# Nearest-neighbour upsampling: one run of 512 rows per partition, two loads and ten stores, and no hold between them

## Chip, cores and metric

One core of one Trainium2 chip. The metric is the time of one execution in microseconds (us); the kernel before takes 199.01 us (median of 3 runs, 198.98 to 199.02). "Span" is the time from the first to the last instruction in a profiled execution, 1.6 to 1.8 us less than the time. Transfer sizes follow the profile: 4096 KB there is 4.194 MB.

## The reference

```python
# x: (16, 64, 64, 64) float32, scale_factor = 2
result = np.zeros((batch, channels, 2 * h, 2 * w), dtype=np.float32)
for i in range(new_h):
    for j in range(new_w):
        result[:, :, i, j] = x[:, :, i // 2, j // 2]
```

Each element is written four times: 16.78 MB are read and 67.11 MB written. As rows, x has 65,536 rows of 64 elements (256 B), and each becomes 256 elements (1 KB) of output.

## The kernel before

The input goes in quarters, 128 rows per partition in each. The last quarter's load is cut, so that 24 rows per partition come as a small piece of their own. VectorE expands 9/16 of a store's rows, ScalarE the rest, and SyncE issues every transfer. Eight stores have 32 rows and four have 64. The **hold**: the first store waits for the last load but one. Its data has been there for some 24 us by then, so this is a wait on purpose.

```python
    M4 = R // (4 * P)                      # 128 rows per partition in a quarter
    slots = [0, 2, 3, 1]
    TAIL = 24
    ...
    for n, slot in enumerate(slots):
        first = n * P * M4
        xt = mem[:, slot * WB : (slot + 1) * WB].rearrange("p (m w) -> p m w", m=M4)
        src = xf[first : first + P * M4, :].rearrange("(p m) w -> p m w", p=P)
        cuts = (0, M4 - TAIL, M4) if n == len(slots) - 1 else (0, M4)
        for lo, hi in zip(cuts, cuts[1:]):
            loads.append(nc.sync.dma_start(out=xt[:, lo:hi], in_=src[:, lo:hi]))
    ...
    def store(part, r0, k, at):
        kv = k * 9 // 16
        ...
        nc.vector.tensor_copy(out=u[:, :kv], in_=expanded(xp[:, r0 : r0 + kv, :]))
        nc.scalar.copy(out=u[:, kv:], in_=expanded(xp[:, r0 + kv : r0 + k, :]))
        dst = of[first : first + P * m, :].rearrange("(p m) w -> p m w", p=P)
        return nc.sync.dma_start(out=dst[:, r0 : r0 + k, :], in_=u)
    ...
    for n, (q, r0) in enumerate(small):
        st = store(q, r0, 32, WX + n % 2 * (WU // 2))
        if n == 0:
            tc.add_manual_dep(st.ins, loads[-2].ins.name, ...,
                reason="stores begin as the loads end")
```

## Time and profile before

| | before |
|---|---|
| time, median of 3 | 199.01 us |
| span | 197.4 us |
| busy: transfers / ScalarE / VectorE | 98.9% / 26% / 20% |
| transfers | 5 loads, 12 stores |

Read the transfers' share first: with 98.9% neither VectorE nor ScalarE can be the bound. Then the landings: how long after its issue each group of transfers has landed. This is the part of the page on issues, with size of one and median time to landing in us:

```profile
out_dram<-mem SPq DMA_DIRECT2D x8, 4096.0 KB, 16.2
mem<-in_x_dram SPq DMA_DIRECT2D x3, 4096.0 KB, 21.4
mem<-in_x_dram SPq DMA_DIRECT2D x1, 3328.0 KB, 38.1
mem<-in_x_dram SPq DMA_DIRECT2D x1, 768.0 KB, 39.4
```

The small last load lands 1.3 us further from its issue than the one before it.

### The profile page before, as it was taken

To read this page: it belongs to the slowest core of one execution; us is meant where nothing else is said; L and a number is where in the kernel's file an instruction comes from. 1 tells how busy PE (TensorE), PEld (TensorE's weight loads), DVE (VectorE), ACT (ScalarE), POOL (GpSimd) and SP (SyncE) were. 2 spreads that over 40 slices of the span, in tenths; PEclk is the share of its full clock that TensorE was granted. 3 is DMA by queue.
4 is the path that set the end of the run, shared out by engine and by line. 5 is a ranking of instruction groups with operands and counts; after the bars stand their busy time and mean duration, and the time that the engine had idled before them with its cause. 6 is when DMAs were issued, how large, how long until landed. Compare 5 with 4: busy or idle time off the path is not lost.

```text
span 197.4 us, 117 instructions
## 1 busy us (share of the span) xinstructions
DVE 40.2 (20%) x12; ACT 51.3 (26%) x13; POOL 0.2 (0%) x4
## 2 busy tenths in 40 slices
DVE  0045000000505059505050007200810091000000
ACT  2047000000505060606079107400840093000000
POOL 0000000000000000000000000000000000000000
DMA  8999999999999999999999999999999999999994
GB/s 319 425 425 425 438 445 418 411 452 451 432 425 438 425 432 432 425 432 425 425 425 425 425 425 425 478 505 438 438 438 438 438 438 425 425 425 425 425 425 212
DMA packets 2448, 83.89 MB, mean 425 GB/s; under 512 B 272, under 2 KB 272, under 8 KB 400
## 3 DMA queue, kind: packets, MB, share of 16 engines
q1 hardware_dynamic: 2448, 83.89, 98.9%
HBM read 16.78 MB, written 67.11 MB: 425 GB/s over the span
## 4 chain that ended last, share of the span: by engine, by line
DMA 71%; ACT 11%; SPq 1%; issue 0%; ACTq 0%
DMA out_dram<-mem 52%; DMA mem<-in_x_dram 19%; ACT mem L140 11%; SPq L124 0%; SPq L142 0%; ACTq L140 0%
## 5 line engine op out<-in xcount | busy, mean ns | idle before, releaser
L140 ACT COPY mem<-mem 128x3584 f32<-128x3584 f32 (+1 forms) x12 | 50.0, 4174 | 112.5 <-DMA out_dram<-mem 102.1
L139 DVE COPY mem<-mem 128x4608 f32<-128x4608 f32 (+1 forms) x12 | 40.2, 3360 | 123.1 <-DMA out_dram<-mem 110.6
L140 ACT ACT_TABLE_LOAD x1 | 1.3, 1283 | 0.8 <-PEq L178 0.8
L178 POOL MEMSET const-bfloat16-1.0<- 128x1 bf16 x1 | 0.1, 102 | 0.0
L178 POOL MEMSET const-uint8-127<- 128x1 uint8 x1 | 0.1, 101 | 0.0
L178 POOL MEMSET const-float32-0.0<- 128x1 f32 x1 | 0.1, 99 | 0.2 <-issue 0.2
L178 POOL MEMSET const-float32-1.0<- 128x1 f32 x1 | 0.1, 98 | 0.0
## 6 DMA issues: line engine op xcount, KB each, us to landing
out_dram<-mem SPq DMA_DIRECT2D x8, 4096.0 KB, 16.2
mem<-in_x_dram SPq DMA_DIRECT2D x3, 4096.0 KB, 21.4
mem<-in_x_dram SPq DMA_DIRECT2D x1, 3328.0 KB, 38.1
mem<-in_x_dram SPq DMA_DIRECT2D x1, 768.0 KB, 39.4
out_dram<-mem SPq DMA_DIRECT2D x4, 32.4
```

Source lines behind the costliest of these rows:

```text
L139: nc.vector.tensor_copy(out=u[:, :kv], in_=expanded(xp[:, r0 : r0 + kv, :]))
L140: nc.scalar.copy(out=u[:, kv:], in_=expanded(xp[:, r0 + kv : r0 + k, :]))
L178: nc = _bacc.Bacc("TRN2", target_bir_lowering=False, num_devices=1)
```

## The change

Its intent: fewer and longer transfers. Each partition owns 512 rows that follow one another, so any cut of its rows is a single run in memory. Two loads of 256 rows (64 KB per partition) replace five, and ten stores of 40 to 56 rows replace twelve. The stores are issued as soon as they are ready and stand in the queue behind the second load; the hold and the small last load go.

```diff
... (views of x and of the output added)
-    M4 = R // (4 * P)
-    slots = [0, 2, 3, 1]
-    TAIL = 24
+    rows = [40, 44, 44, 54, 54, 56, 56, 56, 56, 52]
+    FREE = 79
+    mem = mem_pool.tile([P, WF + R * W], fdt, name="mem")      # R = 512 here
+    xt = mem[:, WF:].rearrange("p (r w) -> p r w", r=R)
... (quarters, cuts and list of loads removed)
+    for lo in range(0, R, R // 2):
+        nc.sync.dma_start(out=xt[:, lo : lo + R // 2], in_=xp[:, lo : lo + R // 2])
... 
+    for n, k in enumerate(rows):
+        size = k * GROW * W
+        at = 0 if n % 2 == 0 else WF + r0 * W - size
...
+        kv = k * 9 // 16
+        nc.vector.tensor_copy(out=u[:, :kv], in_=expanded(r0, r0 + kv))
+        nc.scalar.copy(out=u[:, kv:], in_=expanded(r0 + kv, r0 + k))
+        nc.sync.dma_start(out=op[:, r0 : r0 + k, :], in_=u)
... (store() and its two loops removed)
-        if n == 0:
-            tc.add_manual_dep(st.ins, loads[-2].ins.name, ...)
```

The odd stores are built on top of input rows that are already expanded.

More of the change, by code (lines that the diff above doesn't have):

```diff
@@ L93 @@
     B, C, H, W = x.shape
-    R = B * C * H
+    R = B * C * H // P
     fdt = x.dtype
-    WX = R // P * W
-    WU = 16384
-    mem_pool = ctx.enter_context(tc.tile_pool(name="mem", bufs=1))
-    mem = mem_pool.tile([P, WX + WU], fdt, name="mem")
-    M4 = R // (4 * P)
-    slots = [0, 2, 3, 1]
-    TAIL = 24
-    WB = M4 * W
-    assert M4 * P * 4 == R and 2 * WB == WU
-    xf = x.rearrange("b c h w -> (b c h) w")
-    of = out.rearrange("b c (h hd) w -> (b c h) (hd w)", hd=s)
-    parts = []
@@ L117 @@
-    loads = []
-    for n, slot in enumerate(slots):
-        first = n * P * M4
-        xt = mem[:, slot * WB : (slot + 1) * WB].rearrange("p (m w) -> p m w", m=M4)
-        src = xf[first : first + P * M4, :].rearrange("(p m) w -> p m w", p=P)
-        cuts = (0, M4 - TAIL, M4) if n == len(slots) - 1 else (0, M4)
-        for lo, hi in zip(cuts, cuts[1:]):
-            loads.append(nc.sync.dma_start(out=xt[:, lo:hi], in_=src[:, lo:hi]))
-        parts.append([(xt, first, M4)])
-    def expanded(rows):
-        return rows.unsqueeze(2).unsqueeze(4).to_broadcast(
-            [P, rows.shape[1], s, W, s]
-        )
@@ L132, in store @@
-    def store(part, r0, k, at):
-        xp, first, m = part
-        kv = k * 9 // 16
-        u = mem[:, at : at + k * s * W * s].rearrange(
+    xp = x.rearrange("b c h w -> (b c h) w").rearrange("(p r) w -> p r w", p=P)
+    op = out.rearrange("b c (h hd) w -> (b c h) (hd w)", hd=s).rearrange(
+        "(p r) w -> p r w", p=P
+    )
+    rows = [40, 44, 44, 54, 54, 56, 56, 56, 56, 52]
+    GROW = s * s
+    FREE = 79
+    WF = FREE * GROW * W
+    assert sum(rows) == R
+    mem_pool = ctx.enter_context(tc.tile_pool(name="mem", bufs=1))
@@ new lines, with expanded @@
+    mem = mem_pool.tile([P, WF + R * W], fdt, name="mem")
+    xt = mem[:, WF:].rearrange("p (r w) -> p r w", r=R)
+    for lo in range(0, R, R // 2):
+        nc.sync.dma_start(
+            out=xt[:, lo : lo + R // 2], in_=xp[:, lo : lo + R // 2]
+        )
+    def expanded(r0, r1):
+        return (
+            xt[:, r0:r1].unsqueeze(2).unsqueeze(4).to_broadcast([P, r1 - r0, s, W, s])
+        )
+    r0 = 0
+    before = (0, 0)
+    for n, k in enumerate(rows):
+        size = k * GROW * W
+        at = 0 if n % 2 == 0 else WF + r0 * W - size
+        assert at >= before[1] or at + size <= before[0]
+        before = (at, at + size)
+        u = mem[:, at : at + size].rearrange(
@@ L137, in store @@
             "p (k a w b) -> p k a w b", k=k, a=s, w=W
         )
-        nc.vector.tensor_copy(out=u[:, :kv], in_=expanded(xp[:, r0 : r0 + kv, :]))
-        nc.scalar.copy(out=u[:, kv:], in_=expanded(xp[:, r0 + kv : r0 + k, :]))
-        dst = of[first : first + P * m, :].rearrange("(p m) w -> p m w", p=P)
-        return nc.sync.dma_start(out=dst[:, r0 : r0 + k, :], in_=u)
-    small = [(q, r0) for n in (0, 3) for q in parts[n] for r0 in range(0, q[2], 32)]
-    large = [(q, r0) for n in (1, 2) for q in parts[n] for r0 in range(0, q[2], 64)]
@@ L148 @@
-    for n, (q, r0) in enumerate(small):
-        st = store(q, r0, 32, WX + n % 2 * (WU // 2))
-        if n == 0:
-            tc.add_manual_dep(
-                st.ins,
-                loads[-2].ins.name,
-                mybir.DependencyInfo(
-                    mybir.DependencyClass.Sync, mybir.DependencyReason.DATA
-                ),
-                reason="stores begin as the loads end",
-            )
-    for n, (q, r0) in enumerate(large):
-        store(q, r0, 64, (0, WX)[n % 2])
+        kv = k * 9 // 16
@@ L165 @@
+        nc.vector.tensor_copy(out=u[:, :kv], in_=expanded(r0, r0 + kv))
+        nc.scalar.copy(out=u[:, kv:], in_=expanded(r0 + kv, r0 + k))
+        nc.sync.dma_start(out=op[:, r0 : r0 + k, :], in_=u)
+        r0 += k
 _INS = ['x', 'scale_factor']
```

## The prediction

> **What bounds the kernel now.** I read the page first: the busy shares, the row of DMA in the slices, and the part on DMA queues.
>
> ```profile
> span 197.4 us, 117 instructions
> DVE 40.2 (20%) x12; ACT 51.3 (26%) x13; POOL 0.2 (0%) x4
> ...
> DMA  8999999999999999999999999999999999999994
> GB/s 319 425 425 425 438 445 418 411 452 451 432 425 438 425 432 432 425 432 425 425 425 425 425 425 425 478 505 438 438 438 438 438 438 425 425 425 425 425 425 212
> DMA packets 2448, 83.89 MB, mean 425 GB/s; under 512 B 272, under 2 KB 272, under 8 KB 400
> ...
> q1 hardware_dynamic: 2448, 83.89, 98.9%
> ```
>
> The two engines that compute are busy for a fifth and a quarter of the span. The transfers are busy for 98.9% of it, and in all but the first and the last slice. So the kernel is a queue of transfers. Three things could make it shorter: a hole in the queue, a cost per transfer, or a higher rate. I looked for each.
>
> For that I need a clock of when transfers land. The timeline gives it: a copy that waited for a buffer starts when the store that held the buffer has landed.
>
> ```profile
> 12.49 5.03 DVE L139 COPY mem<-mem 128x4608 f32<-128x4608 f32 x2 [12.49 <-DMA mem<-in_x_dram]
> 39.86 125.06 SPq L142 DMA_DIRECT2D out_dram<-mem  x12
> 51.48 3.18 ACT L140 COPY mem<-mem 128x3584 f32<-128x3584 f32 x1 [32.73 <-DMA out_dram<-mem]
> ...
> 119.60 6.17 ACT L140 COPY mem<-mem 128x7168 f32<-128x7168 f32 x1 [10.09 <-DMA out_dram<-mem]
> ...
> 158.42 4.96 DVE L139 COPY mem<-mem 128x9216 f32<-128x9216 f32 x1 [14.47 <-DMA out_dram<-mem]
> ```
>
> Columns: start, busy time, engine, line, operation, shape, and in brackets the idle time before it with what ended it. The first load (4096 KB, which is 4.194 MB) lands at 12.49. The first store lands at 51.48 and the eighth at 119.60, since the second large expansion waits for that one. The last store is issued at 164.60 (timeline) and takes 32.53 us to land (last transfer piece of the chain in order of time), so it lands at 197.13.
>
> From this I work out three numbers:
> - A 4.194 MB store every (119.60 - 51.48) / 7 = 9.731 us.
> - An 8.389 MB store every (197.13 - 119.60) / 4 = 19.383 us.
> - Two small ones take 2 x 9.731 = 19.462, so a transfer has a fixed part of about 0.08 us; the rest is (19.383 - 0.08) / 8.389 = 2.301 us per MB, or 434.6 GB/s.
>
> The queue's start follows from the first load: 12.49 - 9.73 = 2.76 us. Now the check. If there were no hole anywhere, the end would be 2.76 + 83.886 x 2.301 + 17 x 0.08 = 2.76 + 193.02 + 1.36 = 197.14. The trace has 197.13. At the hold itself: five loads and one store are 20.97 MB, so the first store should land at 2.76 + 48.25 + 0.48 = 51.49; the trace has 51.48. **There is no hole at the hold**, nor elsewhere that I can see. The chain of waits does show 38.12 us of loads and then a store issued at 39.86, but the last load piece (768 KB, issued at 2.2, 39.4 us to landing) lands only at 41.6, so the store was in the queue before the queue ran dry.
>
> **What the Trainium skill says.**
> - "DMA: Bandwidth & Descriptors", section "Where 436 GB/s comes from": the ports of the 16 engines into the core's memory allow 435.2 GB/s. My 434.6 between landings agrees, so there is no rate left to gain.
> - The same page, "Queues, rings and completion order": on each engine descriptors are consumed in ring order. So a store issued while loads are still queued stands behind them and does not take their place. The trace of before agrees in order at least: the small last load landed at 41.6 and the store behind it at 51.48, one store's time later.
> - The same page, "Latency and other measured facts", on row pitch in HBM: with a pitch of 512 KiB from partition to partition copies ran at 207 GB/s, with 2 MiB at 164, where 214 was full. This bears on the change, as below; the trace of before, whose output pitch is 128 KB, can't show it.
> - "SBUF — State Buffer", "Who interferes with whom": DMA doesn't contend with the compute engines. Before agrees: the cadence of 9.73 us is the same for stores that have copies beside them all along.
>
> **The change part by part.**
>
> *Fewer transfers.* 5 loads become 2, 12 stores become 10: 17 transfers become 12. The bytes stay. 5 x 0.08 = 0.4 us less, all on the path, since the queue is the path. That is the whole certain gain.
>
> *No hold.* It takes away a wait that cost nothing (the check above). What happens instead: the first load is now 8.389 MB and lands at 2.76 + 19.30 + 0.08 = 22.1. Copy costs come from the groups by shape:
>
> ```profile
> L140 ACT COPY mem<-mem 128x3584 f32<-128x3584 f32 x8 | 25.3, 3178 | 75.9 <-DMA out_dram<-mem 65.5 <-DMA mem<-in_x_dram 10.4
> L140 ACT COPY mem<-mem 128x7168 f32<-128x7168 f32 x4 | 24.7, 6166 | 36.6 <-DMA out_dram<-mem 36.6
> L139 DVE COPY mem<-mem 128x4608 f32<-128x4608 f32 x8 | 20.4, 2559 | 77.3 <-DMA out_dram<-mem 64.8 <-DMA mem<-in_x_dram 12.5
> L139 DVE COPY mem<-mem 128x9216 f32<-128x9216 f32 x4 | 19.8, 4960 | 45.9 <-DMA out_dram<-mem 45.8
> ```
>
> The number after the bar is the group's busy time, then the mean of one in ns. ScalarE: (6166 - 3178) / 3584 = 0.834 ns per element plus 0.19 us. VectorE: (4960 - 2559) / 4608 = 0.521 ns plus 0.16 us. The first expansion has 40 rows, of which 18 for ScalarE, 18 x 256 = 4608 elements, 4.0 us. The first store is issued at about 26.3, the second (20 rows on ScalarE, 5120 elements, 4.5 us) at 30.8. Both wait in the queue for the second load, which lands at 2.76 + 38.61 + 0.16 = 41.5. So the queue holds 11 to 15 us of work ahead of them.
>
> *Does the queue stay full after that?* An expansion n needs the space of store n - 2, and runs while store n - 1 drains. The tightest case is a 44-row store (5.767 MB, 13.35 us) over the expansion of 54 rows (24 on ScalarE, 6144 elements, 5.3 us): 8 us to spare. The longest expansion (56 rows: 25 on ScalarE, 6400 elements, 5.5 us; 31 on VectorE, 7936 elements, 4.3 us) runs under a store of at least 54 rows, 16.4 us. The new buffers overlap rows of the input that are already expanded; those are waits between the two engines of at most a copy's length, hidden as well. Busy time of the engines hardly moves: 10 instructions each in place of 12, the same elements, so about 50 and 39 us.
>
> *Longer rows, other pitch.* Loads go from 32 KB rows that follow one another without a gap to 64 KB rows with a pitch of 128 KB. Stores go from 32 and 64 KB rows with a pitch of 128 KB to rows of 40 to 56 KB with a pitch of 512 KB. A longer row gains no more than is in the 0.08 above. The pitch is the one thing that could cost.
>
> *Ends.* The first load is still moved ahead of the barrier, and the closing is the same, so the 2.76 at the start and the time outside the span (199.01 - 197.4 = 1.6) stay.
>
> Sum: the queue ends at 2.76 + 193.02 + 12 x 0.08 = 196.7, and the time is 199.01 - 0.4 = 198.6.
>
> **The rivals.**
> 1. *The pitch slows the stores.* If the figure of the skill's page holds for the stores alone, they run at 207 / 214 of their rate: the 67.11 MB take 154.4 us now and would take 5.2 us more, so 203.8, just over 2% slower. For it: the slices show the packets of the engines bunched in time in the large-store stage (one microsecond 1049 GB/s, the next 0, around 128 us), so the engines do walk in step, which is what aliasing needs. Against it: that figure is for loads and stores at the same pitch and with short tiles, and here only the stores have it, a single direction at a time. I give a full cost of 2% or more 0.12, and a part of it 0.15.
> 2. *The hold paid for something*, as its author must have thought: stores in the queue early mix with loads and slow them, or delay the second load. For: it was put in on purpose. Against: ring order, and no copy needs the second load before the sixth expansion (rows 236 to 292), which waits for the fourth store, near 41.5 + 182 x 0.131 MB x 2.301 = 96 us. At most a microsecond.
> 3. *An engine becomes the bound at the start or a copy runs late.* The first expansion starts 10 us later than now. It has 15 us to spare, so it costs nothing; it would have to take four times as long to show.
> 4. *Faster by more than 2%* would need 4 us. The queue has 197.13 - 192.8 (83.886 MB at 435.2 GB/s) = 4.3 us above the port's limit, of which 2.76 is the start. I see no way to it.
>
> **Range and chances.** With 0.73 the time is 198.6 within half a microsecond; the pitch gives a tail upward to 204. I set the prediction a little above the sum, at 198.8, the range from 198.2 to 201.5. Faster 0.01, within 2% 0.87, slower 0.12.
>
> **What would show it right or wrong.** Right: 12 transfers, a DMA share of 98% or more, the first store issued near 26 us and landing near 53.6, landings of 56-row stores every 7.340 x 2.301 + 0.08 = 17.0 us, no slice in the middle below 420 GB/s. The pitch is at work if the 56-row stores land every 17.4 us or more, while the loads still land near 22.1 and 41.5. The hold's rival is at work if the second load lands well after 41.5. A copy is late if SyncE's queue issues a store after the one before it has landed.

## The result and the profile after

The changed kernel takes 199.12 us (median of 6 runs, 199.04 to 199.25), the kernel before 198.96 us in the same rounds. The ratio is 1.0009, with a 95% interval of 0.9996 to 1.0022: the same. A ratio here is the mean time of one kernel's fast runs over that of the other's of the same rounds, so not quite the ratio of the medians. Runs e1 to e4 were made on one chip and e5 to e11 on another, each with the kernel before beside them.

The page of the changed kernel, its lines on the span, busy shares, slices and queue:

```profile
span 197.3 us, 103 instructions
DVE 59.6 (30%) x10; ACT 52.1 (26%) x11; POOL 0.2 (0%) x4
...
GB/s 425 425 425 425 425 425 425 425 282 490 437 439 439 439 439 429 368 538 359 437 460 370 534 372 407 523 372 407 523 372 407 523 372 407 523 372 413 464 432 259
...
q1 hardware_dynamic: 1728, 83.89, 99.1%
```

Its timeline (columns as before):

```profile
25.88 146.81 SPq L139 DMA_DIRECT2D out_dram<-mem  x10
54.38 4.46 ACT L138 COPY mem<-mem 128x5120 f32<-128x5120 f32 x1 [24.04 <-DMA out_dram<-mem]
...
122.19 5.52 ACT L138 COPY mem<-mem 128x6400 f32<-128x6400 f32 x1 [3.08 <-DVE mem L137]
130.61 8.42 DVE L137 COPY mem<-mem 128x7936 f32<-128x7936 f32 x1 [8.51 <-DMA out_dram<-mem]
147.41 5.53 ACT L138 COPY mem<-mem 128x6400 f32<-128x6400 f32 x1 [19.70 <-DMA out_dram<-mem]
147.48 8.42 DVE L137 COPY mem<-mem 128x7936 f32<-128x7936 f32 x1 [8.45 <-DMA out_dram<-mem]
...
164.41 7.88 DVE L137 COPY mem<-mem 128x7424 f32<-128x7424 f32 x1 [8.51 <-DMA out_dram<-mem]
```

Three things are to be seen. The stores run at the predicted pace: 56-row stores land at 130.61, 147.48 and 164.41, 16.9 us apart. But the first store lands at 54.38 and not at the predicted 53.6, so something before it cost 0.7 to 0.8 us. And VectorE takes 8.42 us for 7936 elements, twice what I worked out. ScalarE waits for it twice, some 3.1 us each time (the line at 122.19 is one), but the stores are still in time: the copy that starts at 130.61 is done at 139.03, and the queue has work until the store ahead lands, at 147.4.

Where the 0.8 us went can be read from the windows, here of 1.5 us. A packet is a piece of a transfer; here it is the 64 KB of one partition. It is counted where it starts, so each window below holds the sixteen packets of one round, one per transfer engine. The last two columns are the transfers' share of engine time and GB/s:

```profile
35.00:36.50 1.50, 0.00 (x0) 0.00 (x0) 0.00 (x0) 1.00 1.61 699
37.50:39.00 1.50, 0.00 (x0) 0.00 (x0) 0.00 (x0) 1.00 2.34 699
```

Both windows start the same bytes. The first is a round in the middle of the second load: 1.61 x 1.50 = 2.42 us per packet. The second is that load's last round: 2.34 x 1.50 = 3.51 us. So **the last packets of the loads were stretched by 1.1 us** on average, just before the stores that were waiting behind them. The second load lands late too. The view of the loads' line gives the times from issue to landing of the two loads as least and greatest:

```profile
DMA to landing us min/median/max: 21.8/31.6/41.4
```

The second was issued at 0.8, so it landed at 42.2 where 41.5 was predicted.

### The profile page after: what moved, and what is told of

Read it like the earlier page. It is cut to its first block, busy times and chain, and to the rows that moved or that the text cites. A ratio compares the mean times of both kernels' runs of the same rounds, so it can differ in the third digit from the quotient of the medians.

```text
span 197.3 us, 103 instructions
## 1 busy us (share of the span) xinstructions
DVE 59.6 (30%) x10; ACT 52.1 (26%) x11; POOL 0.2 (0%) x4
## 4 chain that ended last, share of the span: by engine, by line
DMA 67%; DVE 13%; ACT 7%; issue 0%; DVEq 0%; SPq 0%; ACTq 0%
DMA out_dram<-mem 56%; DVE mem L137 13%; DMA mem<-in_x_dram 11%; ACT mem L138 7%; DVEq L137 0%; SPq L139 0%; ACTq L138 0%
## 5 line engine op out<-in xcount | busy, mean ns | idle before, releaser
L137 DVE COPY mem<-mem 128x7936 f32<-128x7936 f32 (+4 forms) x10 | 59.6, 5969 | 112.7 <-DMA out_dram<-mem 90.9
L138 ACT COPY mem<-mem 128x6400 f32<-128x6400 f32 (+4 forms) x10 | 50.8, 5077 | 108.3 <-DMA out_dram<-mem 82.3
```

Of the source, the lines that this page charges most:

```text
L137: nc.vector.tensor_copy(out=u[:, :kv], in_=expanded(r0, r0 + kv))
L138: nc.scalar.copy(out=u[:, kv:], in_=expanded(r0 + kv, r0 + k))
```

## The experiments

**My theory, called Q:** a store that stands in the queue while the last loads still run stretches those loads; the hold avoids this by putting the first store into the queue just as the loads end. **Rivals:** the small last piece is what makes the switch cheap, hold or no hold (C); the hold was idle, as I had predicted (H); the 512 KB pitch of the stores costs time (P).

| run | transfers | time us | kernel before us (same runs) | ratio (95% interval) |
|---|---|---|---|---|
| changed kernel | 12 | 199.12 | 198.96 | 1.0009 (0.9996 to 1.0022) |
| e1, before without hold | 17 | 199.40 | 198.94 | 1.0019 (1.0007 to 1.0032) |
| e2, changed + cut + hold | 13 | 198.75 | 198.94 | 0.9989 (0.9977 to 1.0002) |
| e3, changed + cut | 13 | 199.15 | 198.94 | 1.0009 (0.9997 to 1.0022) |
| e4, changed, even rows | 12 | 199.19 | 198.94 | 1.0012 (0.9998 to 1.0026) |
| e5, changed, unbroken stores | 12 | 199.24 | 198.97 | 1.0016 (1.0002 to 1.0030) |
| e6, changed, stores in four | 42 | 200.58 | 198.97 | 1.0081 (1.0068 to 1.0094) |
| e7, changed + hold of one, no cut | 12 | 205.57 | 198.97 | 1.0334 (1.0318 to 1.0350) |
| e8, changed + hold, cut of 64 rows | 13 | 199.18 | 198.97 | 1.0008 (0.9995 to 1.0021) |
| e9, changed + hold of two, no cut | 12 | 200.01 | 198.98 | 1.0051 (1.0037 to 1.0066) |
| e10, e2 + even rows | 13 | 198.81 | 198.98 | 0.9990 (0.9977 to 1.0003) |
| e11, changed + hold, cut of 12 rows | 13 | 205.45 | 198.98 | 1.0329 (1.0316 to 1.0342) |

### e1: the kernel before without its hold

```diff
-        if n == 0:
-            tc.add_manual_dep(st.ins, loads[-2].ins.name, ...)
```

> The kernel before without the wait of the first store; loads as before, the last piece of 24 rows too. Theory Q (stores that are queued while loads still run stretch the last load packets): the switch from loads to stores loses about 1 us, as in the changed kernel, so the first store lands near 52.5 instead of 51.5 and the time is 199.9 to 200.0. Rival C (the small last piece of the loads is what makes the switch cheap): first store lands at 51.5, time 199.0 within 0.15. Rival H (the hold was simply idle, as I predicted): the same as C here.

Measured: 199.40 us, slower than before by 0.46 us; that is small, but the interval of the ratio lies above 1. The issues show the place (the two load lines that stand above for the kernel before, and the first landing from the timeline):

```profile
mem<-in_x_dram SPq DMA_DIRECT2D x1, 3328.0 KB, 38.0
mem<-in_x_dram SPq DMA_DIRECT2D x1, 768.0 KB, 40.3
...
52.27 3.18 ACT L140 COPY mem<-mem 128x3584 f32<-128x3584 f32 x1 [33.64 <-DMA out_dram<-mem]
```

The small last load took 0.9 us longer to land than in the kernel before; the load ahead of it did not. The first store landed at 52.27 in place of 51.48. So the sign is Q's and the place too, but of the 0.8 us at the first store only about half is left in the time. H is out, and so is C, since the small piece was there.

### e2 and e3: hold and cut put back into the changed kernel, and the cut alone

```diff
-    for lo in range(0, R, R // 2):
-        nc.sync.dma_start(out=xt[:, lo : lo + R // 2], ...)
+    TAIL = 24
+    cuts = (0, R // 2, R - TAIL, R)
+    for lo, hi in zip(cuts, cuts[1:]):
+        loads.append(nc.sync.dma_start(out=xt[:, lo:hi], in_=xp[:, lo:hi]))
 ...
+        if n == 0:                      # e2 only
+            tc.add_manual_dep(st.ins, loads[-2].ins.name, ...)
```

> The changed kernel with both put back: the second load cut into 232 and 24 rows, the first store held until the 232 rows have landed. One transfer more than the changed kernel (0.08 us). Theory Q and rival C both expect the first store to land near 53.4 (the changed kernel: 54.4) and a time of 198.1 to 198.4. Rival H, and a cost that lies in the pitch or the long rows of the loads: 199.1 to 199.3, as the changed kernel.

> The changed kernel with the cut of the second load (232 and 24 rows) but no hold. Theory Q: the switch still loses about 1 us, time 199.1 to 199.3, first store lands near 54.4. Rival C: the cut is enough, 198.1 to 198.4, first store lands near 53.4.

Measured: 198.75 us with the hold (198.66 to 198.78), 199.15 without (198.92 to 199.29). The two differ in the hold alone, and their runs don't overlap. The cut alone gains nothing: e3 takes as long as the changed kernel (199.12). The issues and landings of e2, with the hold, from the page, the timeline and the chain in order of time:

```profile
mem<-in_x_dram SPq DMA_DIRECT2D x1, 7424.0 KB, 38.6
...
mem<-in_x_dram SPq DMA_DIRECT2D x1, 768.0 KB, 40.1
...
53.62 4.46 ACT L139 COPY mem<-mem 128x5120 f32<-128x5120 f32 x1 [23.19 <-DMA out_dram<-mem]
...
96.80 8.42 DVE L138 COPY mem<-mem 128x7936 f32<-128x7936 f32 x1 [12.19 <-DMA out_dram<-mem]
...
164.03 7.89 DVE mem L138
```

The same of e3, without the hold:

```profile
mem<-in_x_dram SPq DMA_DIRECT2D x1, 7424.0 KB, 38.7
...
mem<-in_x_dram SPq DMA_DIRECT2D x1, 768.0 KB, 41.1
...
54.47 4.46 ACT L139 COPY mem<-mem 128x5120 f32<-128x5120 f32 x1 [24.05 <-DMA out_dram<-mem]
...
97.46 8.42 DVE L138 COPY mem<-mem 128x7936 f32<-128x7936 f32 x1 [12.14 <-DMA out_dram<-mem]
...
164.51 7.88 DVE mem L138
```

The small last load lands 1.0 us later without the hold, as in e1. At the first store the hold is 0.85 us ahead, near 97 us it is 0.66 ahead, near 164 us it is 0.48, and in the time 0.40. **So the hold gains 0.85 us at the switch, and about half is given back**: with it, the stores that follow run a little slower, 110.41 us between the first and the last of these landings against 110.04. My estimate of 198.1 to 198.4 for e2 counted only the gain at the switch and was too low.

The windows from 39 to 40 us lie in the small last load, first of e2 and then of e3 (columns as before):

```profile
39.00:40.00 1.00, 0.00 (x0) 0.00 (x0) 0.00 (x0) 1.00 1.02 430
39.00:40.00 1.00, 0.00 (x0) 0.00 (x0) 0.00 (x0) 1.00 1.12 270
```

With the engines as busy, e3 moves 270 GB/s there and e2 430. The packets themselves, read from the packed trace, say the same: the 128 packets of that load take 0.23 us each in e2, and 0.35 us on average and up to 0.65 in e3, which is 0.94 us more for each transfer engine. The packets also show where the gain goes. Those of the 56-row stores (57,344 bytes) take 2.123 us on average in e2 and 2.116 in e3, and the 32-row stores' of the kernel before and e1 1.220 and 1.213. So it is each packet that is 0.3 to 0.6% longer, not a hole between packets. It goes with the switch and not with the hold as such: e8 below has a hold that ends too early, and its 56-row packets take 2.116 us as in e3. Why is open; no run here tells it.

With e1 these runs make a square. Before to e2 is the new layout with the hold in both: 198.94 to 198.75. e1 to e3 is the new layout with no hold in either: 199.40 to 199.15. The layout, which has four transfers fewer here and not five, gains 0.19 to 0.25 us, the hold 0.40 to 0.46, in either combination.

### e8: the first store early by a few microseconds only

```diff
-    TAIL = 24
+    TAIL = 64        # against e2
```

> As the version with the hold, but the last piece of the loads is 64 rows (4.8 us of transfer) in place of 24 (1.8 us), so the first store is in the queue about 4 us before the loads end and not 1 us. Theory Q in its strict form (a store in the queue before the loads' last 50 KB per engine stretches them): the loss is back, first store lands near 54.4, time 199.1. If what matters is only a long lead of 14 us or more: 53.6 and 198.7.

Measured: 199.18 us. The first issue of a store and the first landing:

```profile
36.73 136.22 SPq L140 DMA_DIRECT2D out_dram<-mem  x10
54.63 4.46 ACT L139 COPY mem<-mem 128x5120 f32<-128x5120 f32 x1 [23.95 <-DMA out_dram<-mem]
```

The loss is back in full, although the store joins the queue some 4 us before the loads end. So a lead of 4 us is as bad as one of 15 (e3), and Q holds in its strict form. In e2 the store was issued at 39.53, some 1.4 us before the last load packet ended (40.91 in the packed trace). What a lead between 1.4 and 4 us costs was not tested.

### e7 and e9: the hold without the cut

```diff
-    cuts = (0, R // 2, R - TAIL, R)
+    cuts = (0, R // 2, R)               # against e2
 ...
-        if n == 0:                       # loads[-2]
+        if n == 0:                       # e7, loads[-1];  n < 2 in e9
```

> The changed kernel with the first store held until the whole second load has landed, no small last piece. Theory Q with its cost of issuing: the stretch of the last load packets goes, but the queue runs dry between the landing and the first store packet, about 0.2 us of landing and 1.0 us of issue; so no gain or a small loss against the changed kernel, 199.1 to 199.6, first store landing 54.3 to 54.8. If any hold is good, 198.7 as with the cut.

e7 missed by far: 205.57 us. The reason is the order in which the build placed the stores, not the hold. SyncE's list of transfers in the built program of e7 (in elements per partition) begins:

```text
L119 DMACopy mem<-in_x_dram 128x16384
L119 DMACopy mem<-in_x_dram 128x16384
L139 DMACopy out_dram<-mem 128x11264
L139 DMACopy out_dram<-mem 128x10240
```

The 44-row store (11264 elements) goes ahead of the held 40-row store; the trace agrees, its first store is one of 45,056 bytes per partition, issued at 30.50. It stretches the loads as ever (2.23 in the window from 37.5 to 39, so 3.35 us per packet), and the third expansion, which needs the room of the 40-row store, starts 13 us late, at 67.70. The queue then runs dry. The slices of e7:

```profile
GB/s 412 412 412 412 412 412 451 373 425 425 412 499 402 0 283 487 526 358 456 413 424 445 348 534 360 541 361 462 439 360 541 360 462 439 360 541 348 502 335 335
```

The slice with 0 is that hole. e9 is the mended run: the first two stores wait, so that none goes ahead.

> The hold without a small last piece, mended: the first two stores wait for the whole second load, so that the second store cannot go ahead of the first. Theory Q: no load packet is stretched, but the queue is empty from the end of the loads to the first store packet, about 1.2 us (0.2 of landing, 1.0 of issue) in place of the stretch of 1.0: 199.1 to 199.6, first store lands at 54.3 to 54.8. If the small last piece has no use: 198.7 and 53.6.

Measured: 200.01 us, worse than expected by some 0.4. The first store landed at 54.72, as expected, so the rest was lost after the switch; the packets of the 56-row stores take 2.122 us here, as in e2, and 2.116 in the changed kernel. The windows of e9 (columns as above):

```profile
35.00:36.50 1.50, 0.00 (x0) 0.00 (x0) 0.00 (x0) 1.00 1.61 699
37.50:39.00 1.50, 0.00 (x0) 0.00 (x0) 0.00 (x0) 1.00 1.61 699
39.00:42.00 3.00, 0.00 (x0) 0.00 (x0) 0.00 (x0) 1.00 0.00 0
```

The last round of the loads has the same share as the one in the middle: **with no store in the queue, nothing is stretched.** Those packets start by 39.0 and last 2.42 us, so they end by 41 or so; no store packet starts before 42.0. At the first landing that hole costs 0.34 us more than the stretch (54.72 against 54.38). This is what the small last piece is for: it lets the wait end about as long before the loads end as a store takes from its issue to its first packet (in e2 1.0 us, from 39.53 to 40.54 in the packed trace).

### e11: a last piece of 12 rows

```diff
-    TAIL = 24
+    TAIL = 12        # against e2
```

> As the version with hold and cut of 24 rows, but the last piece is 12 rows (0.9 us of transfer). The first store's packets can start about 1.0 us after its wait ends, so theory Q expects a hole of a few tenths of a microsecond at most: first store lands at 53.6 to 54.0, time 198.7 to 199.0.

Measured: 205.45 us. It is no test of the size: as in e7, the second store was placed ahead of the first (first store issue at 30.37, third expansion at 67.79). The best size of the last piece stays open: only 24 and 64 rows were tested.

### e5: the stores' pitch

```diff
-        nc.sync.dma_start(out=op[:, r0 : r0 + k, :], in_=u)
+        dst = of[P * r0 : P * (r0 + k), :].rearrange("(p k) w -> p k w", p=P)
+        nc.sync.dma_start(out=dst, in_=u)     # rows in wrong places, on purpose
```

> The changed kernel, but each store writes one unbroken stretch of the output (a row pitch of 40 to 56 KB in place of 512 KB); the rows land in the wrong places, on purpose. Rival P (the 512 KB pitch slows the stores): faster than the changed kernel, 1 us or more, and the 56-row stores land closer together than 16.9 us. If the pitch costs nothing: 199.1 within 0.2, 16.9 us between landings.

Measured: 199.24 us, not faster, and the 56-row stores land 16.9 us apart as with the pitch of 512 KB. VectorE's copies, which wait for these landings:

```profile
130.70 8.42 DVE L137 COPY mem<-mem 128x7936 f32<-128x7936 f32 x1 [8.49 <-DMA out_dram<-mem]
...
147.59 8.42 DVE L137 COPY mem<-mem 128x7936 f32<-128x7936 f32 x1 [8.46 <-DMA out_dram<-mem]
```

The changed kernel has 130.61 and 147.48. P is out.

### e6: the fixed cost of a transfer

```diff
-        nc.sync.dma_start(out=op[:, r0 : r0 + k, :], in_=u)
+        for j in range(4):
+            lo, hi = k * j // 4, k * (j + 1) // 4
+            nc.sync.dma_start(out=op[:, r0 + lo : r0 + hi, :], in_=u[:, lo:hi])
```

> The changed kernel with each store issued as four transfers of a quarter of its rows: 30 transfers more, the same bytes and the same places. The fixed cost that I read from the cadence (0.08 us per transfer) makes it 30 x 0.08 = 2.4 us slower than the changed kernel, 201.5. If the fixed cost is no cost of a transfer but noise of my reading, it stays at 199.1[...].

Measured: 200.58 us, 1.46 us above the changed kernel for 30 transfers, so 0.05 us each. Each transfer brings its own packets with it, so the 0.05 is for a transfer and its packets together. The cost is real and hardly more than half of the 0.08 that I read from the cadence. The difference of two cadences, 19.46 and 19.38, was too small a number to rest on.

### e4 and e10: even row counts for VectorE

```diff
-        kv = k * 9 // 16
+        kv = k * 9 // 32 * 2
```

> The changed kernel with VectorE's share rounded down to an even number of rows (30 of 56, 28 of 52, in place of 31 and 29). If VectorE's slow copies (8.42 us for 7936 elements) come from the odd row count, its copies of 30 rows take 4.16 us as those of the 54-row stores do and its busy time falls from 59.6 to about 39 us; if they come from the length or the place in memory, they stay above 8 us. The time stays at 199.1 within 0.15 in both cases, since the copies are hidden.

> The candidate to beat both kernels: the changed kernel with the hold, the cut of 24 rows and even row counts for VectorE. The same time as the version with hold and cut alone, 198.6 to 198.8, below the kernel before (198.95); VectorE's copies of 30 rows take 4.16 us. A repeat of that result on its own runs.

Measured: e4 199.19 us, e10 198.81 us, the times of the changed kernel and of e2. VectorE's groups by shape, in the changed kernel:

```profile
L137 DVE COPY mem<-mem 128x7936 f32<-128x7936 f32 x4 | 33.7, 8420 | 37.0 <-DMA out_dram<-mem 37.0
L137 DVE COPY mem<-mem 128x7680 f32<-128x7680 f32 x2 | 8.3, 4160 | 19.1 <-DMA out_dram<-mem 19.1
```

and in e4:

```profile
L137 DVE COPY mem<-mem 128x7680 f32<-128x7680 f32 x6 | 25.0, 4160 | 68.8 <-DMA out_dram<-mem 68.8
```

One row less (30 in place of 31) at the same place halves the copy, and the copy of 29 rows in the changed kernel is slow too (7.88 us) although it is shorter than that of 30. So the odd count is the cause, not the length or the place. The time doesn't move, because the copies are hidden.

**The version to keep.** e2 and e10 have the lowest medians, 0.2 us below the kernel before, in two separate sets of runs; each interval still touches 1, so against the kernel before this is likely and not certain. Against the changed kernel with the cut alone the gain of the hold is clear.

## Why the prediction was right or wrong

The range held: 199.12 lies within 198.2 to 201.5, and the two kernels agree within 2%. The sum beneath did not. It said 0.4 us faster; the medians of the same rounds say 0.16 slower, with an interval that still includes no change. That the range held is in part luck: it reached so far up for the pitch, which cost nothing, and the time missed the "198.6 within half a microsecond" that had 0.73. By its own steps:

- **The bound.** Right. The transfers fill the span in both kernels, and the time follows what happens in their queue. One piece of evidence is put too strongly: the stores with "copies beside them all along" have ScalarE at work for 3.2 us of each 9.7. What shows that the copies don't slow the stores is e4, where VectorE works 21 us less and the time is the same.
- **Fewer transfers, "5 x 0.08 = 0.4 us less".** Right mechanism, size too large: e6 measured 0.05 us per transfer, so an estimate of 0.25 us for five. The square gives 0.19 to 0.25 for the layout with four fewer, which fits 4 x 0.05 = 0.2; that the layout gains by nothing else was not shown apart. The 0.08 also rests on a misreading: the 32.53 us belong to the store issued at 125.79, which landed at 158.33, and the last store landed at 197.04 by the packed trace, not at 197.13. With 197.04 the same subtraction gives 0.10, with the copies' starts at 119.60 and 158.41 it gives 0.06. So the check of 197.14 against 197.13 is worth less than it seems; the one at the hold stands without that landing: 2.76 + 5 x 9.73 = 51.4 against 51.48.
- **No hold, "a wait that cost nothing".** This step failed. It was true that the hold left no hole in the queue. From this I concluded that nothing would be lost without it, and I leaned on ring order: a store behind the loads can't take their place. It doesn't take their place, but it stretches them. The hold is worth 0.40 to 0.46 us (e1 against before, e2 against e3). I had this as the second rival, "at most a microsecond", and had named its sign, a second load that lands well after 41.5; it landed at 42.2.
- **Together**: -0.25 for five transfers fewer and +0.40 to +0.46 for the hold make +0.15 to +0.2. The measured +0.16 fits. The change gained a little over half of the 0.4 us that I had forecast, and lost more than that at the switch from loads to stores.
- **Copies hidden.** Right in effect, wrong in size for VectorE: "about 50 and 39 us" became 50.8 and 59.6, because I took 31 and 29 rows at the pace of even counts. The room in the queue was wide enough for twice the time.
- **The pitch, the first rival.** It didn't come: stores keep their pace with it (16.9 us) and without it (e5).
- **A sign that I chose badly.** "No slice in the middle below 420 GB/s": slices went down to 282 at the switch and to 359 among the stores, while the queue was full. Packets of 2 us that are counted where they start make slices of 4.9 us uneven. The landings were the better sign.

## What to carry to other kernels

When the transfers are the bound, a wait without a hole can still be there for a reason: compare how long the transfers on either side of it take, not only whether the queue is empty. The busy share doesn't show it (99.0% in e2 and in e3 alike). Where a queue turns from loads to stores, let the first store come as the last load ends (here 1.4 us before), neither several microseconds early nor after it; a small last load whose predecessor releases the store does this. Check the order in which the build places the stores, since holding one may let the next go ahead.

## What the Trainium skill lacked or had wrong

- "DMA: Bandwidth & Descriptors", "Queues, rings and completion order", tells that descriptors are consumed in ring order, and neither it nor, as far as I found, any other page tells what a store queued behind loads costs them: the last load packets took 3.51 us in place of 2.42 (changed kernel), and the first store landed 0.85 us later (e3 against e2). Why, inside the transfer engines, these runs don't show.
- The same page, "Anatomy of one DMA — SWDGE (gpsimd) path", gives a fixed cost of about 2.0 us for each transfer that GpSimd issues. It has no figure for one transfer more in a queue of SyncE that is kept full: 0.05 us here (e6).
- The same page, "Latency and other measured facts", has a slower rate for a pitch of 512 KiB in copies between HBM tensors. For stores alone from the core's memory no cost of that pitch appeared: 16.9 us per 56-row store with it and without it (e5).
- "VectorE: DVE Perf Modes", "Mode 2×_2P", allows an odd outermost dimension if it is equal for source and destination. The copy of 31 rows has 31 rows on both sides as written and ran at half the pace (8.42 us, and 4.16 us for 30 rows). In the record of that instruction in the trace the destination is one run of 7936 elements and only the source is 31 x 2 x 64 x 2, so the two may be neither equal nor both even as the engine sees them, and then the page's rule would fit. That reading was not tested; what the page lacks is that equal counts in the kernel's text need not be equal in the instruction.
